# Token rows, their squares and small tables pinned in the instruction order, and transposed operands fetched four k-tiles at a time, in a one-core encoder block

## Chip, core and metric

The kernel runs on one core of one Trainium2 chip. The metric is the device time of one execution in microseconds; three runs give a median. A profiled execution beside them gives the span of the instructions, the busy time of each engine and the trace.

The engines are TensorE (PE; its weight loads are PEld), VectorE (DVE), ScalarE (ACT), GpSimd (POOL) and SyncE (SP). SP and ACT issue the transfers of this kernel; a transfer stands in the instruction stream of the engine that issues it, in that engine's order.

## What is computed

One layer of an encoder block on 256 tokens of width 2048 in float32, cut to what matters:

```python
h = rms_norm(x, g_mix)
proj = h @ w_in                      # q/k/v of mixers A and B, q of mixer C, three gates
oa = dilated windows (3 groups x 2 heads, relative bias), merged by their denominators
ob = grouped-query attention (6 query heads, 2 key/value heads), axial rotary
mkv = rms_norm(mem, g_mem) @ w_mem_kv    # 256 memory tokens -> keys, values of mixer C
oc = cross attention of 4 heads into mkv
merged = sum over branches of sigmoid(gate) * (o_branch @ w_branch)
x = x + merged @ w_o
hf = rms_norm(x, g_ffn) @ w_ffn_in
x = x + (silu(hf[..., :D_FF]) * hf[..., D_FF:]) @ w_ffn_out
```

`rms_norm` divides each token's row by the root of its mean square and multiplies by a gain per channel. The kernel takes these apart. The gain per channel is multiplied into the transposed operand (channels on partitions); the factor per token is applied to the product afterwards. So a product of `mem` can begin before the sums of squares of its rows are known; only what is made from the product needs them.

## The kernel before

**Products.** Every matrix product goes through `product(src, lhs, nk, head, beside)`. It makes 256 tokens x 512 output columns in two PSUM banks (128 tokens each) from `nk` k-tiles of 128 channels. Weights come from memory by SP (`load`, L139 to L148) into one of three buffers `raw` of four k-tiles. `split` (L72) turns a raw float32 tile into two float32r parts: ACT rounds it to `hi`, DVE computes `lo = src - hi`. For weights these are `whi` and `wlo`, four buffers each, two k-tiles per buffer. Each k-tile takes six matmuls, three for each half of the tokens: hi x hi, hi x lo, lo x hi (L172 to L174).

**Transposed operands.** `load_T` (L179) makes the left operand of the products from `memT` or `xT`, which lie transposed in memory. `get(k)` fetches two k-tiles (256 KB) on ACT's queue into `rawT`, which has two buffers, and splits them with the channel gain (L78 on ACT, L79 on DVE). The product asks for them through `lhs(k)`.

**Side work.** Beside the products, generators ("jobs") are advanced by `tick()`, which is called after each k-tile. A job yields the number of k-tiles after which it wants to go on; at most one job advances per tick. The jobs of the opening are:

- `row_sums` (L198): loads the token rows in four tiles `rows` of 128 x 1024 (512 KB each) by SP, squares each on ACT with a sum along the row (L206), and from the sums makes the factor per token (`row_scale`, a chain of small DVE operations). It adds its name to `known`.
- `constants` (L241): three small tables by SP, `gh` (head gains), `rope`, `relb`.
- `fetch` (L249): asks for all of `xT` in steps of two k-tiles, ahead of the first product that reads it.
- `take_slots` (L289): takes a finished product out of PSUM: squares per head (`sq`), then, when the row factors are `known`, the scaled heads `y`, gains, rotary, transposes (`hT`) and splits.
- `biases` and `attend`: tables of relative bias, and the attention of each head.

**Order.** The opening runs two products of `memT` with the two column blocks of `w_mem` (16 k-tiles each), then eight products of `xT` with `w_qkv`. The sums of the mem rows start at k-tile 6 of the first product, those of the x rows at k-tile 0 of the first `w_qkv` product, with pace 3:

```python
first = product(a["w_mem"][0], memT, KT, (1, 1) + (2,) * 7, {6: row_sums(a["mem"], r_m, 3, "mem")})
start(constants())
start(take_slots(first, MEM_SLOTS[:4], r_m, "mem", nc.vector))
start(fetch(xT, 2))
```

The written order is not the order on the chip. The kernel is traced with `schedule_with_timeline_sim=True`: after tracing, a scheduler orders each engine's instructions by a simulated timeline and keeps only the dependences. An instruction that needs nothing but a free buffer, such as a load, can be placed far ahead of where it was written. `tc.keep_in_program_order(ins)` adds one edge: `ins` stays behind the instruction that was traced just before it on the same engine. It adds no wait for that instruction's end, and it does not keep later instructions from passing.

**Buffers.** The pool `mid` has five slots of 4 KB per partition with the common tag `s4`; `rows`, `y`, `sq`, `rot`, `pT`, `row` and later `sg`, `sa` and `junk` share them. The two buffers of `rawT` lie in the pool `wp` and hold 2 KB per partition each.

Of the kernel before, what the change touches and what calls it, by code (L numbers as in the profile page):

```python
# [11 lines left out]
F32 = mybir.dt.float32  # L12
F32R = mybir.dt.float32r
I32 = mybir.dt.int32
AF = mybir.ActivationFunctionType
# [3 lines left out]
P = 128  # L19
S = 256  # L20
T = S // P
D = 2048
KT = D // P
HD = 128
# [12 lines left out]
BUCKETS, MAX_DIST = 32, 1024  # L37
# [13 lines left out]
def encoder_block(ctx: ExitStack, tc: tile.TileContext, a: dict, out: bass.AP):  # L51
    nc = tc.nc
    const = ctx.enter_context(tc.tile_pool(name="const", bufs=1))
    wp = ctx.enter_context(tc.tile_pool(name="wp", bufs=3))
    big = ctx.enter_context(tc.tile_pool(name="big", bufs=11))
    mid = ctx.enter_context(tc.tile_pool(name="mid", bufs=5))
    small = ctx.enter_context(tc.tile_pool(name="small", bufs=4))
    dram = ctx.enter_context(tc.tile_pool(name="dram", bufs=1, space=bass.MemoryType.DRAM))
    pmm = ctx.enter_context(tc.tile_pool(name="pmm", bufs=4, space=bass.MemoryType.PSUM))
# [2 lines left out]
    def s8(shape, name, dt=F32R, pool=None):  # L62
        return (pool or big).tile(shape, dt, name=name, tag="s8")

    def s4(shape, name, dt=F32):
        return mid.tile(shape, dt, name=name, tag="s4")

    def at_bank(name):
        return pat.tile([P, NC], F32, name=name, tag="at")


    def split(hi, lo, src, scale=None):  # L72

        if scale is None:
            nc.scalar.activation(hi, src, AF.Copy)  # L75
            nc.vector.tensor_sub(lo, src, hi.bitcast(F32))  # L76
        else:
            nc.scalar.activation(hi, src, AF.Copy, scale=scale)  # L78
            nc.vector.scalar_tensor_tensor(lo, src, scale, hi.bitcast(F32), op0=ALU.mult, op1=ALU.subtract)  # L79
# [33 lines left out]
    def advance(job):  # L113

        try:
            lag = next(job[1])
            job[0] = now[0] + (lag or 1)
            return lag is not None
        except StopIteration:
            side.remove(job)  # L120
            return True

    def start(steps):

# [14 lines left out]
    def load(src, k0, nk):  # L139

        raw = wp.tile([P, LOAD, NC], F32, name="raw")
        if nk % PK:
            c = k0 % PK * NC
            nc.sync.dma_start(out=raw[:, 0], in_=src[k0 // PK][:, c:c + NC])
        else:
            nc.sync.dma_start(out=raw[:, :nk].rearrange("p (u k) n -> p u (k n)", k=PK),
                              in_=src[k0 // PK:(k0 + nk) // PK].rearrange("u p n -> p u n"))
        return raw  # L148

    def product(src, lhs, nk, head=(), beside={}):  # L150


        ps = [pmm.tile([P, NC], F32, name="mm") for _ in range(T)]
        k0 = 0
        while k0 < nk:
            n = head[0] if head else min(LOAD, nk - k0)
            head = head[1:]
            if k0 in beside:
                start(beside[k0])
            lhs(k0)  # L160
            raw = load(src, k0, n)
            for b in range(0, n, PK):
                m = min(PK, n - b)
                hi = wp.tile([P, PK, NC], F32R, name="whi", bufs=4)
                lo = wp.tile([P, PK, NC], F32R, name="wlo", bufs=4)
                split(hi[:, :m], lo[:, :m], raw[:, b:b + m])
                for i in range(m):
                    k = k0 + b + i
                    xh, xl = lhs(k)
                    for t in range(T):  # L170
                        c = slice(t * P, (t + 1) * P)
                        nc.tensor.matmul(ps[t], lhsT=xh[:, c], rhs=hi[:, i], start=(k == 0), stop=False)  # L172
                        nc.tensor.matmul(ps[t], lhsT=xh[:, c], rhs=lo[:, i], start=False, stop=False)  # L173
                        nc.tensor.matmul(ps[t], lhsT=xl[:, c], rhs=hi[:, i], start=False, stop=(k == nk - 1))  # L174
                    tick()
            k0 += n
        return ps

    def load_T(src, g, tag):  # L179

        tiles = [s8([P, 4, 2, S], tag) for _ in range(KT // 4)]
        have = set()

        def get(k):
            k0 = k // 2 * 2
            tl = tiles[k // 4]
            if k0 not in have:
                have.add(k0)
                raw = wp.tile([P, 2, S], F32, name="rawT", bufs=2)
                nc.scalar.dma_start(out=raw, in_=src[k0 // 2].rearrange("p (k s) -> p k s", s=S))  # L190
                for i in range(k0, k0 + 2):
                    split(tl[:, i % 4, 0], tl[:, i % 4, 1], raw[:, i - k0], g[:, i:i + 1])
            return tl[:, k % 4, 0], tl[:, k % 4, 1]
        return get

# [2 lines left out]
    def row_sums(src, r, pace, name):  # L198

        ss = small.tile([P, T, 2], F32, name="rss", bufs=1)  # L200
        for t in range(T):
            for h in range(2):
                rows = s4([P, D // 2], "rows")
                nc.sync.dma_start(out=rows, in_=src[t * P:(t + 1) * P, h * (D // 2):(h + 1) * (D // 2)])
                yield pace
                nc.scalar.activation(rows, rows, AF.Square, accum_out=ss[:, t, h:h + 1])  # L206
        sr = small.tile([P, T], F32, name="ss", bufs=1)
        nc.vector.tensor_reduce(sr, ss, axis=AX.X, op=ALU.add)
        row_scale(sr, r)
        known.add(name)  # L210

    def transposed(src, dst, g=None):

        for h in range(2):
            tp = at_bank("tp")
            for k in range(2):
                for t in range(T):
                    nc.tensor.transpose(tp[:, k * S + t * P:k * S + (t + 1) * P],  # L218
                                        src[t][:, (2 * h + k) * P:(2 * h + k + 1) * P], ident)
# [17 lines left out]
    gh = const.tile([P, 6, HD], F32, name="gh")  # L237
    rope = const.tile([P, 2, T, HD // 2], F32, name="rope")
    relb = const.tile([P, A_HEADS], F32, name="relb")

    def constants():  # L241
        v = a["g_heads"]
        nc.sync.dma_start(out=gh, in_=bass.AP(tensor=v.tensor, offset=v.offset, ap=[[0, P], [HD, 6], [1, HD]]))
        yield 1
        nc.sync.dma_start(out=rope, in_=a["rope"])
        nc.vector.memset(relb[:64], NEG)
        nc.sync.dma_start(out=relb[:BUCKETS], in_=a["rel_bias"])

    def fetch(get, pace):  # L249
        for k in range(0, KT, 2):  # L250
            get(k)
            yield pace
# [173 lines left out]
    scales = const.tile([P, 3, 2, T], F32, name="scales")  # L426
    r_m, r_x, r_f = (scales[:, i] for i in range(3))
    memT = load_T(a["memT"], gT[:, 1], "memT")
    xT = load_T(a["xT"], gT[:, 0], "xT")
    memT(0)  # L430
    first = product(a["w_mem"][0], memT, KT, (1, 1) + (2,) * 7, {6: row_sums(a["mem"], r_m, 3, "mem")})
    start(constants())
    start(take_slots(first, MEM_SLOTS[:4], r_m, "mem", nc.vector))
    start(fetch(xT, 2))
    start(take_slots(product(a["w_mem"][1], memT, KT, (2,) * 8), MEM_SLOTS[4:], r_m, "mem"))
    oT = [s8([P, 4, 2, S], f"oT{i}") for i in range(3)]
    ol = lambda k: (oT[k // 4][:, k % 4, 0], oT[k // 4][:, k % 4, 1])
    for c in range(8):
        sums = {} if c else {0: row_sums(a["x"], r_x, 3, "x")}
        start(take_slots(product(a["w_qkv"][c], xT, KT, beside=sums), SLOTS[4 * c:4 * c + 4], r_x))  # L440
        if c == 0:
            start(biases())
# [28 lines left out]
    x = [s8([P, D], f"x{t}", F32) for t in range(T)]  # L471
# [20 lines left out]
    for c0, c1 in ((0, 6), (6, KF // 4)):  # L492
        hT = []
        for n in range(c0, c1):
            ap = product(a["w_ffn_a"][n], x1l, KT)
# [7 lines left out]
            tl = s8([P, 2, 4, S], "hT", pool=tail if n % 6 < 4 and n < 6 or n > 8 else None)  # L503
# [91 lines left out]
```

## Time and profile before

| | |
|---|---|
| runs | 1437.47, 1437.15, 1437.45 us; median 1437.45 |
| profiled execution | 1438.22 us, span of its instructions 1436.4 us |
| busy in the span | PE 1416.7, PEld 1170.0, DVE 781.2, ACT 667.2, POOL 78.8 us |
| moved by DMA | 276.98 MB, mean 193 GB/s |
| granted TensorE clock, mean | 0.998 |
| instructions | 16231 |

Times in rows of the profile are microseconds from the start of the span. A timeline row reads: start, duration, engine (an engine with a q, such as SPq, is its sequencer, here issuing a transfer), line, operation, output<-inputs, count; in brackets the idle time of the engine before it and what ended that. A row of a table by stage reads: stretch, length, busy time and number of instructions of PE, PEld, DVE, ACT and POOL, the granted TensorE clock, the mean busy share of the DMA engines, GB/s. A row of waits reads: who waited, for whom, total us, times, longest. A DMA row reads: what, queue, count, KB each, median us from issue to landing. A duration of a matmul is longer than the distance to the next one, since matmuls are pipelined.

### The profile page before, as it was taken

How to read it: one execution, taken by the hardware profiler on the slowest of the kernel's cores; microseconds unless marked ns; L12 is line 12 of the kernel's file. 1: busy time of each engine (PE TensorE's matmuls, PEld its weight loads, DVE VectorE, ACT ScalarE, POOL GpSimd, SP SyncE). 2: the span in 40 equal slices, each digit the busy share in tenths (PEclk: the TensorE clock that was granted, in tenths of full speed). 3: DMA queues.
4: the chain of work that ended last, by engine and by line, in shares of the span. 5: the costliest groups of instructions: out<-in, count | busy, mean ns of one | idle time of the engine just before them, and what ended most of it. 6: DMA issues, size and time to landing. Idle time of an engine off the chain costs nothing.

```text
span 1436.4 us, 16231 instructions
## 1 busy us (share of the span) xinstructions
PE 1416.7 (99%) x6422; PEld 1170.0 (81%) x6422; DVE 781.2 (54%) x912; ACT 667.2 (46%) x860; POOL 78.8 (5%) x146
## 2 busy tenths in 40 slices
PE   6999999999999999999999999999999999999998
PEld 4778788888888888888888888888888888888887
DVE  5677766744555555555644555545444445554543
ACT  6676555644444444444444444444333444444432
POOL 0013642200000000000000000000000000000000
PEclk9999999999999999999999999999999999999999
DMA  8876445465555556555555555565555555556562
GB/s 294 282 248 204 147 153 173 160 222 197 196 192 194 176 189 213 184 187 177 183 197 186 194 177 204 176 205 177 203 179 203 187 194 179 202 177 204 192 218 88
DMA packets 75772, 276.98 MB, mean 193 GB/s; under 512 B 5232, under 2 KB 7792, under 8 KB 75440
## 3 DMA queue, kind: packets, MB, share of 16 engines
q1 hardware_dynamic: 73248, 271.73, 56.0%
q10 hardware_dynamic: 2448, 4.22, 0.8%
q8 instruction: 50, 0.82, 0.2%
q14 instruction: 26, 0.21, 0.0%
HBM read 273.05 MB, written 2.88 MB: 192 GB/s over the span
## 4 chain that ended last, share of the span: by engine, by line
PE 92%; DMA 3%; POOL 2%; ACT 1%; issue 1%; DVE 1%; SPq 0%; ACTq 0%; DVEq 0%; POOLq 0%
PE mm L173 29%; PE mm L172 29%; PE mm L174 29%; PE tp L218 1%; DMA rawT<-in_xT 1%; DMA rows<-in_x 1%; DMA rows<-in_mem 1%; POOL rot L337 1%; POOL rot L340 1%; POOL rtmp L338 1%; ACT whi L75 0%; PE pT L396 0%; ACT rows L206 0%; PE hT L346 0%; POOL y L320 0%
## 5 line engine op out<-in xcount | busy, mean ns | idle before, releaser
L76 DVE TENSOR_TENSOR wlo<-raw,whi 128x1024 fp32r<-128x1024 f32 (+1 forms) x497 | 614.7, 1239 | 584.9 <-ACT whi L75 582.6
L75 ACT ACTIVATE whi<-raw 128x1024 fp32r<-128x1024 f32 (+1 forms) x497 | 525.5, 1061 | 642.6 <-PE mm L174 616.6
L174 PE MATMUL mm<-whi,x1T 128*128 128x512 f32 x704 | 274.8, 390 | 0.0
L172 PE MATMUL mm<-whi,x1T 128*128 128x512 f32 x704 | 274.8, 390 | 0.0
L173 PE MATMUL mm<-wlo,x1T 128*128 128x512 f32 x704 | 274.1, 389 | 0.0
L173 PE MATMUL mm<-wlo,xT 128*128 128x512 f32 x640 | 250.2, 391 | 1.0 <-DVE wlo L76 1.0
L172 PE MATMUL mm<-whi,xT 128*128 128x512 f32 x640 | 250.5, 392 | 0.1
L174 PE MATMUL mm<-whi,xT 128*128 128x512 f32 x640 | 249.5, 391 | 0.0
L173 PEld LDWEIGHTS mm<-wlo,x1T 128*128 128x128 f32 x704 | 132.2, 188 | 27.2
L174 PEld LDWEIGHTS mm<-whi,x1T 128*128 128x128 f32 x704 | 132.2, 188 | 27.1
L172 PEld LDWEIGHTS mm<-whi,x1T 128*128 128x128 f32 x704 | 132.2, 188 | 26.9
L173 PEld LDWEIGHTS mm<-wlo,xT 128*128 128x128 f32 x640 | 120.2, 188 | 26.1 <-DVE wlo L76 1.4
L172 PEld LDWEIGHTS mm<-whi,xT 128*128 128x128 f32 x640 | 120.1, 188 | 25.3 <-issue 0.8
L174 PEld LDWEIGHTS mm<-whi,xT 128*128 128x128 f32 x640 | 120.2, 188 | 24.4
L173 PE MATMUL mm<-wlo,hT 128*128 128x512 f32 x352 | 137.8, 391 | 0.0
L172 PE MATMUL mm<-whi,hT 128*128 128x512 f32 x352 | 137.7, 391 | 0.0
L174 PE MATMUL mm<-whi,hT 128*128 128x512 f32 x352 | 137.0, 389 | 0.0
L172 PEld LDWEIGHTS mm<-whi,hT 128*128 128x128 f32 x352 | 66.1, 188 | 14.4
L174 PEld LDWEIGHTS mm<-whi,hT 128*128 128x128 f32 x352 | 66.1, 188 | 14.3
L173 PEld LDWEIGHTS mm<-wlo,hT 128*128 128x128 f32 x352 | 66.1, 188 | 13.5
L173 PE MATMUL mm<-wlo,mT 128*128 128x512 f32 x128 | 50.8, 397 | 0.0
L172 PE MATMUL mm<-whi,mT 128*128 128x512 f32 x128 | 50.5, 395 | 0.0
(123 smaller groups left out, 997.5 us busy)
## 6 DMA issues: line engine op xcount, KB each, us to landing
raw<-in_w_gate SPq DMA_DIRECT2D x48, 1024.0 KB, 5.0
raw<-in_w_ffn_a SPq DMA_DIRECT2D x44, 1024.0 KB, 5.0
raw<-in_w_ffn_b SPq DMA_DIRECT2D x44, 1024.0 KB, 5.0
raw<-in_w_ffn_out SPq DMA_DIRECT2D x44, 1024.0 KB, 5.0
raw<-in_w_qkv SPq DMA_DIRECT2D x32, 1024.0 KB, 5.1
raw<-in_w_o SPq DMA_DIRECT2D x16, 1024.0 KB, 5.0
raw<-in_w_br SPq DMA_DIRECT2D x8, 1024.0 KB, 4.9
raw<-in_w_mem SPq DMA_DIRECT2D x15, 512.0 KB, 4.9
```

Of the source, the lines that this page charges most:

```text
L75: nc.scalar.activation(hi, src, AF.Copy)
L76: nc.vector.tensor_sub(lo, src, hi.bitcast(F32))
L172: nc.tensor.matmul(ps[t], lhsT=xh[:, c], rhs=hi[:, i], start=(k == 0), stop=False)
L173: nc.tensor.matmul(ps[t], lhsT=xh[:, c], rhs=lo[:, i], start=False, stop=False)
L174: nc.tensor.matmul(ps[t], lhsT=xl[:, c], rhs=hi[:, i], start=False, stop=(k == nk - 1))
L218: nc.tensor.transpose(tp[:, k * S + t * P:k * S + (t + 1) * P], src[t][:, (2 * h + k) * P:(2 * h + k + 1) * P], ident)
L337: nc.gpsimd.tensor_mul(ov[:, :, :, c], xv[:, :, :, c], cs[0])
L338: nc.gpsimd.tensor_mul(tmp[:, :n], xv[:, :, :, 1 - c], cs[1])
L340: op(ov[:, :, :, c], ov[:, :, :, c], tmp[:, :n])
```

## The change

Five things, all in the opening:

1. `ordered` (that is, `tc.keep_in_program_order`) is put around the loads of the token rows, their squares, the three tables and the fetches of the transposed operands.
2. `row_sums` is written so that a row tile's load is issued one step ahead of the square of the tile before it; pace 4 in place of 3. The mem sums start at k-tile 8 in place of 6. `constants` yields 8 k-tiles after its first table in place of 1.
3. `get` fetches a quad of four k-tiles as two transfers of 256 KB into one `s4` slot `rawT`; the splits of each k-tile stay where they were. With `fetch=True` it only fetches.
4. A job `ahead` fetches quads in advance: of `memT` from k-tile 2 with pace 3, of `xT` from the end of the first product with pace 4. `fetch` begins 4 k-tiles later.
5. `mid` has six slots in place of five; the two `rawT` buffers in `wp` go.

```diff
-    mid = ctx.enter_context(tc.tile_pool(name="mid", bufs=5))
+    mid = ctx.enter_context(tc.tile_pool(name="mid", bufs=6))
+    ordered = tc.keep_in_program_order
@@ product
-            if k0 in beside:
-                start(beside[k0])
+            for job in beside.get(k0, ()):
+                start(job)
@@ load_T
-        have = set()
-        def get(k):
-            k0 = k // 2 * 2
-            tl = tiles[k // 4]
+        raws, have = {}, set()
+        def get(k, fetch=False):
+            k0, q = k // 2 * 2, k // 4
+            tl = tiles[q]
+            if q not in raws:
+                raw = raws[q] = s4([P, 4, S], "rawT")
+                for u in range(2):
+                    ordered(nc.scalar.dma_start(out=raw[:, 2 * u:2 * u + 2],
+                                                in_=src[2 * q + u].rearrange("p (k s) -> p k s", s=S)))
+            if fetch:
+                return
             if k0 not in have:
                 have.add(k0)
-                raw = wp.tile([P, 2, S], F32, name="rawT", bufs=2)
-                nc.scalar.dma_start(out=raw, in_=src[k0 // 2].rearrange("p (k s) -> p k s", s=S))
                 for i in range(k0, k0 + 2):
-                    split(tl[:, i % 4, 0], tl[:, i % 4, 1], raw[:, i - k0], g[:, i:i + 1])
+                    split(tl[:, i % 4, 0], tl[:, i % 4, 1], raws[q][:, i % 4], g[:, i:i + 1])
@@ row_sums
-        for t in range(T):
-            for h in range(2):
-                rows = s4([P, D // 2], "rows")
-                nc.sync.dma_start(out=rows, in_=...)
-                yield pace
-                nc.scalar.activation(rows, rows, AF.Square, accum_out=ss[:, t, h:h + 1])
+        parts = [(t, h) for t in range(T) for h in range(2)]
+        rows = []
+        for i in range(len(parts) + 1):
+            if i < len(parts):
+                t, h = parts[i]
+                rows.append(s4([P, D // 2], "rows"))
+                ordered(nc.sync.dma_start(out=rows[i], in_=...))
+            if i:
+                t, h = parts[i - 1]
+                ordered(nc.scalar.activation(rows[i - 1], rows[i - 1], AF.Square, accum_out=ss[:, t, h:h + 1]))
+            yield pace
@@ constants: the three loads in ordered(...); yield 8 for yield 1
@@ fetch
+        yield 4
@@ opening
+    def ahead(get, pace):
+        for k in range(0, KT, 4):
+            get(k, True)
+            yield pace
+
     memT(0)
-    first = product(..., (1, 1) + (2,) * 7, {6: row_sums(a["mem"], r_m, 3, "mem")})
+    first = product(..., (1, 1) + (2,) * 7, {2: [ahead(memT, 3)], 8: [row_sums(a["mem"], r_m, 4, "mem")]})
     start(constants())
     start(take_slots(first, MEM_SLOTS[:4], r_m, "mem", nc.vector))
+    start(ahead(xT, 4))
     start(fetch(xT, 2))
...
-        sums = {} if c else {0: row_sums(a["x"], r_x, 3, "x")}
+        sums = {} if c else {0: [row_sums(a["x"], r_x, 4, "x")]}
```

More of the change, by code (lines that the diff above doesn't have):

```diff
@@ L200, in row_sums @@
         ss = small.tile([P, T, 2], F32, name="rss", bufs=1)
-        for t in range(T):
-            for h in range(2):
-                rows = s4([P, D // 2], "rows")
-                nc.sync.dma_start(out=rows, in_=src[t * P:(t + 1) * P, h * (D // 2):(h + 1) * (D // 2)])
-                yield pace
-                nc.scalar.activation(rows, rows, AF.Square, accum_out=ss[:, t, h:h + 1])
+        parts = [(t, h) for t in range(T) for h in range(2)]
[4 more added lines that the diff above has]
+                rows.append(s4([P, D // 2], "rows"))
+                ordered(nc.sync.dma_start(out=rows[i],
+                                          in_=src[t * P:(t + 1) * P, h * (D // 2):(h + 1) * (D // 2)]))
+            if i:
+                t, h = parts[i - 1]
+                ordered(nc.scalar.activation(rows[i - 1], rows[i - 1], AF.Square, accum_out=ss[:, t, h:h + 1]))
+            yield pace
         sr = small.tile([P, T], F32, name="ss", bufs=1)
@@ L242, in constants @@
         v = a["g_heads"]
-        nc.sync.dma_start(out=gh, in_=bass.AP(tensor=v.tensor, offset=v.offset, ap=[[0, P], [HD, 6], [1, HD]]))
-        yield 1
-        nc.sync.dma_start(out=rope, in_=a["rope"])
+        ordered(nc.sync.dma_start(out=gh, in_=bass.AP(tensor=v.tensor, offset=v.offset, ap=[[0, P], [HD, 6], [1, HD]])))
+        yield 8
+        ordered(nc.sync.dma_start(out=rope, in_=a["rope"]))
         nc.vector.memset(relb[:64], NEG)
-        nc.sync.dma_start(out=relb[:BUCKETS], in_=a["rel_bias"])
+        ordered(nc.sync.dma_start(out=relb[:BUCKETS], in_=a["rel_bias"]))
     def fetch(get, pace):
+        yield 4
         for k in range(0, KT, 2):
@@ L429, in encoder_block @@
     xT = load_T(a["xT"], gT[:, 0], "xT")
+    def ahead(get, pace):
+        for k in range(0, KT, 4):
+            get(k, True)
+            yield pace
     memT(0)
-    first = product(a["w_mem"][0], memT, KT, (1, 1) + (2,) * 7, {6: row_sums(a["mem"], r_m, 3, "mem")})
+    first = product(a["w_mem"][0], memT, KT, (1, 1) + (2,) * 7, {2: [ahead(memT, 3)], 8: [row_sums(a["mem"], r_m, 4, "mem")]})
     start(constants())
     start(take_slots(first, MEM_SLOTS[:4], r_m, "mem", nc.vector))
+    start(ahead(xT, 4))
     start(fetch(xT, 2))
```

## Prediction

> **What bounds the kernel now.** I read the page's busy table and its slices first, then the table by stage for the whole span, then TensorE's own waits, then the timeline of the first 70 us with all engines and queues.
>
> ```profile
> PE 1416.7 (99%) x6422; PEld 1170.0 (81%) x6422; DVE 781.2 (54%) x912; ACT 667.2 (46%) x860; POOL 78.8 (5%) x146
> PE   6999999999999999999999999999999999999998
> ...
> 0.00:62.00 62.00, 49.54 (x194) 38.91 (x195) 37.92 (x82) 38.49 (x68) 0.70 (x6) 0.94 0.85 285
> 62.00:140.00 78.00, 76.88 (x365) 61.61 (x365) 54.17 (x100) 50.58 (x101) 19.09 (x33) 1.00 0.72 234
> 140.00:180.00 40.00, 38.27 (x197) 32.07 (x195) 30.33 (x52) 21.64 (x52) 25.52 (x37) 1.00 0.47 157
> 180.00:400.00 220.00, 220.00 (x1054) 184.34 (x1053) 131.12 (x170) 113.92 (x174) 33.53 (x71) 1.00 0.54 184
> ...
> 1200.00:1400.00 200.00, 200.00 (x895) 165.40 (x894) 98.47 (x88) 83.80 (x85) 0.00 (x0) 1.00 0.58 198
> ```
>
> Columns of the stage rows: stretch, its length, busy PE, weight load, DVE, ACT, POOL with counts, granted clock, DMA share, GB/s. From 180 to 1400 us (first and last of six rows) TensorE has no idle time: nothing that the edit does there can gain, and there is slack on every other engine. The opening is different: 62 us hold 49.54 us of TensorE, at a clock of 0.94. Two stages behind it lack 1.1 and 1.7 us. So the case is decided in the first two products (both w_mem column blocks, 32 k-tiles).
>
> ```profile
> PE mm L172 <- ACT memT L78: 11.9, 2, 6.2
> PE hT L346 <- POOL rot L340: 1.7, 2, 1.4
> PE mm L173 <- DVE wlo L76: 1.0, 1, 1.0
> PE mm L174 <- DVE memT L79: 0.2, 1, 0.2
> ...
> 2.12 3.04 SPq L204 DMA_DIRECT2D rows<-in_mem  x4
> 5.30 1.48 SPq L146 DMA_DIRECT2D raw<-in_w_mem  x2
> 8.51 0.34 ACTq L190 DMA_DIRECT2D rawT<-in_memT  x1
> 9.71 1.04 ACT L206 ACTIVATE rows<-rows 128x1024 f32<-128x1024 f32 x1
> 13.36 0.61 PE L174 MATMUL mm<-whi,memT 128*128 128x512 f32 x2
> 14.17 1.06 ACT L206 ACTIVATE rows<-rows 128x1024 f32<-128x1024 f32 x1 [3.33 <-DMA rows<-in_mem]
> 16.27 1.04 ACT L206 ACTIVATE rows<-rows 128x1024 f32<-128x1024 f32 x1
> 17.30 1.99 ACT L75 ACTIVATE whi<-raw 128x1024 fp32r<-128x1024 f32 x2
> 19.20 0.90 ACT L78 ACTIVATE memT<-rawT,gT 128x256 fp32r<-128x256 f32 x2
> 19.75 0.80 PE L172 MATMUL mm<-whi,memT 128*128 128x512 f32 x1 [5.77 <-ACT memT L78]
> ```
>
> Of the 11.9 us, 6.2 are the start (first operands must land) and 5.77 are one hole. The rows show its making. In the code the row sums start at k-tile 6, but SP issued all four row loads at 2.12 us, ahead of the weights of k-tiles 4 to 7 (5.30). ACT's queue has the squares early as well: it sits 3.33 us for the second row tile, squares until 17.30, splits two weight tiles, and only then splits memT for k-tile 4, which TensorE wanted at 13.97.
>
> The hole has a second price, the clock.
>
> ```profile
> 14.00:19.00 5.00, 0.00 (x0) 0.00 (x0) 1.36 (x8) 4.83 (x8) 0.00 (x0) 0.84 1.01 389
> 20.00:22.00 2.00, 1.82 (x4) 0.93 (x4) 1.97 (x8) 0.09 (x1) 0.00 (x0) 0.50 0.49 113
> 22.00:24.00 2.00, 1.94 (x5) 1.56 (x6) 0.93 (x6) 1.06 (x2) 0.00 (x0) 0.50 0.71 252
> 24.00:26.00 2.00, 2.00 (x10) 1.64 (x9) 1.98 (x4) 1.74 (x3) 0.00 (x0) 0.94 0.71 284
> ```
>
> For some 4.5 us behind the hole the granted clock is 0.50: 4 and 5 matmuls begin in 2 us where 10 do at 0.94. The start has the same half pace, 0.43 us between two starts, though the clock column says 1.00 there; that one stays.
>
> ```profile
> 7.18 0.63 PE L172 MATMUL mm<-whi,memT 128*128 128x512 f32 x1
> ...
> 7.61 0.63 PE L173 MATMUL mm<-wlo,memT 128*128 128x512 f32 x1
> ```
>
> **The change, part by part.** First the ceiling. The steady pace of these products:
>
> ```profile
> 54.78 0.39 PE L172 MATMUL mm<-whi,memT 128*128 128x512 f32 x1
> 61.36 0.39 PE L174 MATMUL mm<-whi,memT 128*128 128x512 f32 x1
> 61.58 0.39 PE L172 MATMUL mm<-whi,xT 128*128 128x512 f32 x1
> ```
>
> Thirty matmuls start between 54.78 and 61.58, 0.2267 us each, so a k-tile of six takes 1.360 us. K-tile 3 ends with the pair that starts at 13.36; the next could start at about 13.81. The 28 remaining mem k-tiles without a hole would bring the first xT matmul to 13.81 + 28 x 1.360 = 51.9 instead of 61.58. **Ceiling: 9.7 us**: 5.8 hole, about 2.1 clock, the rest waits under 1 us that follow it.
>
> *Rows and squares pinned.* No instruction is removed or added. Row tile 0 is now issued behind the weights of k-tiles 6 and 7, its square stands four k-tiles later, and so on; the last mem square moves from 17 us to behind k-tile 24 of 32.
>
> ```profile
> L206 ACT ACTIVATE rows<-rows x8: 1039/1048/1086, 9.7 to 75.5; 128x1024 f32<-128x1024 f32 x8
> L206 ACT ACTIVATION_READ_ACCUMULATOR rows<-rows x8: 185/186/225, 10.7 to 76.4; 128x1 f32 x8
> rows<-in_mem SPq DMA_DIRECT2D x4, 512.0 KB, 8.0
> ```
>
> A square with its read costs about 1.14 us of ACT (next start to start), once in four k-tiles of 5.44 us. What hides it: per two k-tiles (2.72 us) ACT has one weight split (1.06) and one memT pair (0.90), so 3.9 us in four k-tiles, and 5.1 with the square. That is 94% of ACT while memT is being split; afterwards it is easy. If the cover goes, a square costs TensorE at most its 1.14 us, four of them 4.6. A row load takes 8.0 us to land and has four k-tiles plus the queue's lead of three weight buffers; SP does not wait on it, only ACT at the square.
>
> *Small tables pinned.* gh, rope and relb (0.5 MB in all, 384 + 128 + 0.8 KB) leave the 7.7 to 11 us stretch and are issued between the products. Before, they lay among full-rate transfers; at the 389 GB/s of the row from 14 us they free 1.3 us of transfer there. I count that inside the ceiling. Nobody needs gh before the first y has been scaled:
>
> ```profile
> 60.13 0.86 ACT L313 ACTIVATE y<-mm,hf 128x128 f32<-128x128 f32 x3
> ```
>
> *Transposed operands by fours.* Still eight transfers of 256 KB per operand, now two per quad, both on ACT's queue. Bytes and issues do not change. What changes is where a fetch stands: quads 1, 2 and 3 of memT go behind the weight splits of k-tiles 3, 7 and 11, and the splits that need them follow almost directly. This is the price I cannot read off, so I bound it by landings:
>
> ```profile
> rawT<-in_memT ACTq DMA_DIRECT2D x1, 256.0 KB, 6.1
> rawT<-in_memT ACTq DMA_DIRECT2D x8, 256.0 KB, 4.3
> rawT<-in_xT ACTq DMA_DIRECT2D x1, 256.0 KB, 2.6
> ```
>
> (slowest of the stretch of interest, median of eight, fastest.) With 4.3: quad 1 issued at 8.5 (as the fetch in the rows above) lands 12.8, split 0.5 later, needed 13.81: 0.3 allowed for the vector half. ACT then has two memT pairs and a weight split (2.8 us, its last part overlapped by the issue), so quad 2 leaves at 15.0, lands 19.3, usable 19.8; needed at 19.25 (+0.3): 0.3 to 0.5. Quad 3 leaves at 22.5 if ACT splits in written order, lands 26.8, usable 27.3, needed at 25.5: 1.8; if ACT does the weight splits while it waits for quad 2, as it did at 17.30, nothing. I take 1.0. Sum 1.8. With 2.6 the sum is about 0. With 6.1 in written order it grows from quad to quad: 1.3, then 2.85, then 3.9, in all 8.0. I take the median: it comes from fetches among weight loads alone, as these will be, while 6.1 had row tiles and tables in flight with it.
>
> xT's quads start 16 k-tiles ahead of use, paced by four; no cost. They share the six slots with rows, y, sq; counting lifetimes in written order I get at most six live at once, so I count no slot wait (the rival below does). The sixth slot later costs and gains nothing: TensorE is full there. POOL's queue gets nothing and loses nothing.
>
> *Transfers as a second ceiling.* By the first xT matmul must have landed: memT 2.1, w_mem 8.4, mem rows 2.1, xT 2.1, tables 0.5, first w_qkv load 1.05 MB: 16.3 MB. The opening row moved 285 GB/s at a share of 0.85, so 335 at 1.0: 48.6 us, plus 2.5 until the first bytes, 51.1. That is under 51.9, with hardly a microsecond to spare; I put 0.4 us of weight waits on it.
>
> Sum: 9.7 - 1.8 - 0.4 = **7.5 us**. The later waits (1.1 us around 65 us, 1.7 around 150) I leave as they are: the first came from a burst of row loads that is now spread, the second from POOL's rotation, which moves along. The profiled execution took 1438.22 us around a span of 1436.4; it becomes 1430.7 around 1428.9. It lies 0.77 above the median of 1437.45, so the median becomes 1430.0.
>
> **The rivals.**
> *A: fetches wait in full (6.1 us, written order).* For: the fetch at 8.51 took 6.1, and row tiles 0 and 1 still travel next to quads 2 and 3. Against: the four row loads that filled the engines then are gone. Gain 9.7 - 8.0 = 1.7, so 1435.8. Its last hole, 3.9 us, lies between the 0.99 us idle at 65 us that cost no clock and the 5.77 that did; if it does, 2.1 more: 1437.9, no change.
>
> ```profile
> 65.91 0.50 PE L173 MATMUL mm<-wlo,xT 128*128 128x512 f32 x1 [0.99 <-DVE wlo L76]
> ```
>
> The Trainium skill ("TensorE: Matmul & The Clock Gate", Part 1) has the clock halve after an idle window of about 3.4 us. By it a hole of 2.85 would be spared and one of 3.9 could be hit; no row here lies between 0.99 and 5.77.
>
> *B: fetches land fast (2.6).* For: the row tiles and tables no longer stand in front. Stalls near 0, and the 65 us wait goes as well: 9.7 + 1.0 less 0.4 of weights, 10.3, so 1427.2. Against: the DMA share is still 1.01 between 14 and 19 us in the row above. The Trainium skill ("DMA: Bandwidth & Descriptors", Queues, rings and completion order) says that each DMA engine takes turns between queues packet by packet, so a fetch on ACT's queue would not stand behind SP's backlog but have half the rate: 0.26 MB at 0.2 MB per us is 1.3 us above the bare latency, an estimate that leads to B. The trace speaks against: 6.1 us at 8.51.
>
> *C: a slot wait blocks a queue (slower).* Fetches used to have two slots of their own; now an xT fetch on ACT's queue can wait for a slot held by y, freed only by the head transposes. Everything on ACT stands behind it. ACT leads TensorE by at most four weight tiles, so three more when it stops: 3 x 2.72 = 8.2 us of cover. It costs more than it gains by 0.2% when the wait exceeds 8.2 + 7.5 + 2.9 = 18.6 us; a wait from k-tile 20 to 37 (23 us) would give 1437.45 - 7.5 + 15 = 1445. For: y is held across the w_mem[1] product. Against: six slots suffice by my count.
>
> *D: it doesn't do what it says.* A pin keeps an instruction behind its predecessor, but others can still pass it; if the order of ACT's splits ends up as poor as before, the hole stays, with transfers merely shifted: 1437, within 0.2%. Against: a square can't pass its predecessor, and it was squares that made the hole.
>
> **How the numbers follow.** 0.2% is 2.9 us, about what a measurement tells from no change; the bounds are 1434.6 and 1440.3. Forecast (1428.5 to 1432.5) 0.52; B (below 1428.5) 0.18; A 0.18, of which 0.10 with only some of its waits ends under 1434.6 and 0.08 above; D 0.05; C 0.07. Faster: 0.52 + 0.18 + 0.10 = 0.80; same: 0.08 + 0.05 = 0.13; slower 0.07. The range goes from B's 1427.2 to A's 1435.8, leaving about 0.07 below and 0.13 above.
>
> **What would show it.** Right: row loads at or after 6.8 us on SP's queue; no square on ACT before about 14 us; the 5.77 us hole gone and one stretch of half pace only, the first, as now (0.43 us between starts); the first xT matmul at 54 (51.9 + 2.2); small holes, if any, at k-tiles 8 and 12, charged to memT, with rawT transfers behind them. Wrong: holes above 2 us charged to memT (A), no half clock and xT at 52 (B), an xT fetch or row load whose issue stands for many microseconds with ACT or SP idle behind it (C), squares still ahead of k-tile 8's splits (D).

## The result, and the profile after

The changed kernel takes 1445.03 us (median of 1444.14 to 1447.34) against 1437.46 before: ratio 1.0053, 95% interval 1.0035 to 1.0070. It is 7.6 us slower, where 7.5 us faster was forecast. The profiled execution took 1444.70 us around a span of 1442.9, 6.5 more than before.

The table by stage first (columns as before):

```profile
0.00:62.00 62.00, 48.94 (x192) 38.76 (x192) 38.35 (x80) 40.30 (x67) 0.70 (x6) 0.97 0.87 294
62.00:140.00 78.00, 72.93 (x322) 57.87 (x322) 45.59 (x84) 42.67 (x87) 23.25 (x38) 0.96 0.70 227
140.00:180.00 40.00, 38.25 (x209) 31.64 (x208) 33.20 (x62) 25.84 (x58) 19.41 (x32) 1.00 0.41 134
180.00:400.00 220.00, 220.00 (x1056) 184.31 (x1057) 132.12 (x176) 115.16 (x179) 32.87 (x71) 1.00 0.52 182
```

From 180 us on TensorE is as full as before. The first 62 us hold about as little TensorE work as before, and the stage from 62 to 140 now lacks 5.1 us where it lacked 1.1. TensorE's waits, and the two holes in its timeline:

```profile
PE mm L174 <- ACT memT L80: 10.1, 2, 6.4
PE mm L174 <- DVE V L81: 7.9, 1, 7.9
PE hT L361 <- POOL rot L355: 1.4, 2, 0.9
```

```profile
29.39 0.79 PE L174 MATMUL mm<-whi,memT 128*128 128x512 f32 x1 [3.61 <-ACT memT L80]
67.00 0.76 PE L174 MATMUL mm<-whi,xT 128*128 128x512 f32 x1 [7.90 <-DVE V L81]
```

The old hole of 5.77 us at 14 us is gone. There is one of 3.61 at k-tile 12, and one of 7.90 in front of the first `w_qkv` product. The second does not wait for an operand: `V L81` reads the product `w_mem[1]` out of PSUM. A product needs two of four PSUM banks; the two `w_mem` products held all four. TensorE goes on 0.14 us after a pair of these reads ends; seven of the eight reads by VectorE are done then, which by the program's order empties one of that product's two banks, and the last comes later:

```profile
66.06 0.80 DVE L81 SCALAR_TENSOR_TENSOR V<-mm,scales,V 128x128 fp32r<-128x128 f32 x2
68.83 0.35 DVE L81 SCALAR_TENSOR_TENSOR V<-mm,scales,V 128x128 fp32r<-128x128 f32 x1 [1.98 <-ACT V L80]
```

Behind the hole the clock is halved:

```profile
59.00:67.00 8.00, 0.10 (x1) 0.03 (x1) 7.62 (x22) 5.43 (x13) 0.00 (x0) 0.78 1.00 311
67.00:69.00 2.00, 2.00 (x5) 1.61 (x6) 0.17 (x1) 1.80 (x7) 0.38 (x1) 0.50 1.01 412
69.00:71.00 2.00, 2.00 (x8) 1.58 (x7) 0.18 (x1) 0.00 (x0) 2.00 (x1) 0.68 0.94 336
```

Eight matmuls take the 3.43 us from 67.00 to 70.43 in place of 1.81: 1.6 us more. Why the banks were held is read from SP's, ACT's and VectorE's timelines, here in order of time:

```profile
11.10 0.42 SPq L215 DMA_DIRECT2D rows<-in_mem  x1
19.49 0.90 SPq L215 DMA_DIRECT2D rows<-in_mem  x2
20.54 0.33 SPq L257 DMA_DIRECT2D gh<-in_g_heads  x1
34.28 0.42 SPq L215 DMA_DIRECT2D rows<-in_mem  x1
...
43.76 1.05 ACT L219 ACTIVATE rows<-rows 128x1024 f32<-128x1024 f32 x1
45.03 0.15 DVE L222 TENSOR_REDUCE ss<-rss 128x2 f32<-128x4 f32 x1
55.95 0.16 DVE L109 COPY scales<-rs_y 128x2 f32<-128x2 f32 x1
57.99 0.16 DVE L322 TENSOR_TENSOR hss<-hss,scales 128x8 f32<-128x8 f32 x1
65.98 0.16 DVE L324 TENSOR_TENSOR hf<-rs_y,scales 128x8 f32<-128x8 f32 x1
66.37 2.17 ACT L328 ACTIVATE y<-mm,hf 128x128 f32<-128x128 f32 x8
```

And four of these points in the kernel before, where the fourth row tile was issued by 5.2 us:

```profile
16.27 1.04 ACT L206 ACTIVATE rows<-rows 128x1024 f32<-128x1024 f32 x1
22.77 0.17 DVE L107 COPY scales<-rs_y 128x2 f32<-128x2 f32 x1
48.63 0.16 DVE L307 TENSOR_TENSOR hss<-hss,scales 128x8 f32<-128x8 f32 x1
57.45 0.17 DVE L309 TENSOR_TENSOR hf<-rs_y,scales 128x8 f32<-128x8 f32 x1
```

The last mem square moved from 16.3 to 43.8 us. The factor per token (`scales`) came at 56.0 in place of 22.8, the factor per head (`hf`) at 66.0 in place of 57.5. The chain for the head factor begins with the row `hss`, the first reader of the row factor. Without the head factor `y`, which empties the first product, cannot run. `V`, which empties the second, needs only the row factor; that was there at 56.0, but the second product itself ended at 59.1, and then its reads were drawn out among weight splits until 66.9. So TensorE, done with the second product at 59.1, found no free bank. Each of the two chains is about a dozen VectorE operations of 0.16 us, but they take 11 and 8 us; VectorE's timeline has weight and xT splits between them.

In sum: the first xT matmul 5.4 us later (67.00 against 61.58), 1.6 us of half clock behind it, less the old 0.99 us wait at 65 us: 6.0 of the 6.5 us.

### The profile page after: what moved, and what is told of

Read it like the earlier page. It is cut to its first block, busy times and chain, and to the rows that moved or that the text cites. A ratio compares the mean times of both kernels' runs of the same rounds, so it can differ in the third digit from the quotient of the medians.

```text
span 1442.9 us, 16232 instructions
## 1 busy us (share of the span) xinstructions
PE 1418.7 (98%) x6422; PEld 1171.2 (81%) x6422; DVE 780.7 (54%) x912; ACT 668.9 (46%) x860; POOL 76.2 (5%) x146
## 4 chain that ended last, share of the span: by engine, by line
PE 90%; DMA 4%; DVE 3%; POOL 1%; ACT 1%; issue 1%; SPq 0%; ACTq 0%; DVEq 0%; POOLq 0%
PE mm L175 29%; PE mm L174 29%; PE mm L176 29%; DMA raw<-in_w_mem 2%; DVE wlo L78 1%; PE tp L232 1%; DMA rawT<-in_memT 1%; ACT whi L77 0%; DMA rawT<-in_xT 0%; ACT y L328 0%; PE pT L411 0%; DVE pr L401 0%; DMA relb<-in_rel_bias 0%; DMA flat<-row 0%; PE hT L361 0%
```

## The experiments

**Theory 1:** the mem factors come too late, and the banks stay held. **Theory 2:** pinned row loads hold up the weights on SP's queue. **Theory 3:** the fetches by fours and the shared slots cost the time. The first four kernels part them.

*mem_factor_given* takes the need for the factor away:

```diff
+    dummy = const.tile([P, 2, T], F32, name="dummy")
+    nc.vector.memset(r_m, 1.0)
+    known.add("mem")
...
-    8: [row_sums(a["mem"], r_m, 4, "mem")]
+    8: [row_sums(a["mem"], dummy, 4, "sums")]
```

> The changed kernel, but the row factor of the mem tokens is set to one at the start and nothing waits for the sums of the mem rows; their loads, squares and chain stay and write a table that nobody reads (left out: the true factor). Theory 1 (the mem factor comes late, so neither pair of product banks is free when the first w_qkv product is due): the 7.9 us hole in front of it and the 1.6 us at half clock behind it go, about 1435.5 us; the 3.6 us hole inside the first product stays. Theory 2 (pinned row loads hold up the weight loads on SP's queue): nothing changes there, 1443 or more. Theory 3 (fetches by fours and shared slots): the same, 1443 or more.

Measured: 1435.01 us, ratio 0.9974 (0.9964 to 0.9984). There is no hole in front of the first xT matmul at 58.2 us; a 4.19 us hole inside the first product is left (10.0 less the 5.8 of the start, in the row below). The head factor in VectorE's timeline, and TensorE's waits:

```profile
51.57 0.17 DVE L324 TENSOR_TENSOR hf<-rs_y,scales 128x8 f32<-128x8 f32 x1
```

```profile
PE mm L174 <- ACT memT L80: 10.0, 2, 5.8
PE hT L361 <- POOL rot L355: 3.2, 2, 1.7
```

Ten microseconds (1445.0 against 1435.0) hang on the mem factor alone; the row loads stood where they stood. Theory 1 holds for the large hole, and theories 2 and 3 do not explain it.

*sums_from_6_pace_3*:

```diff
-    8: [row_sums(a["mem"], r_m, 4, "mem")]
+    6: [row_sums(a["mem"], r_m, 3, "mem")]
```

> The changed kernel with the mem sums started at k-tile 6 with pace 3, as before, in place of 8 and 4; all pins and the fetches by fours stay. Written order has the factor known after k-tile 18 in place of 28. Theory 1: ten k-tiles or 13.6 us earlier is more than the 7.9 us that were short, so the large hole goes: 1434 to 1437 us. Theory 2: the row loads stand earlier among the weights, 1445 to 1448. Theory 3: no change, 1445.

Measured: 1435.51 us, ratio 0.9987 (0.9973 to 1.0000). (The written place is k-tile 21, not 18: the new `row_sums` yields once more before the factor.) Its profiled execution took 1443.6 us, 8 above the median, so its trace is not set beside the others here. Start and pace alone are worth 9.5 us, which is the size of the large hole with its half clock (7.9 + 1.6).

The change in two halves, *rows_part_alone* (pins, new `row_sums`, tables; operands still by twos) and *quads_alone* (the new `load_T`, `ahead`, six slots; old `row_sums` and `constants`). Each takes the lines of the change that it names:

```diff
 rows_part_alone, against the kernel before
+ ordered(...) on row loads, squares, tables; square one step behind the load; constants: yield 8
-    {6: row_sums(a["mem"], r_m, 3, "mem")}
+    {8: [row_sums(a["mem"], r_m, 4, "mem")]}
 quads_alone, against the kernel before
-    mid bufs=5, rawT: 2 x [P, 2, S] in wp
+    mid bufs=6, rawT: [P, 4, S] in s4, ordered fetches, ahead(memT, 3), ahead(xT, 4), fetch: yield 4
```

> The kernel before with only the part on rows and tables (pins on row loads, squares and tables, loads one step ahead, start 8, pace 4); operands fetched by twos into two slots of their own, five shared slots. Theory 1: the loss is all here, with the hole in front of the first w_qkv product: 1442 to 1447 us. Theory 2: likewise 1442 to 1447, but with the holes inside the two w_mem products, charged to weights. Theory 3: no loss, 1430 to 1437.

> The kernel before with only the fetches by fours (four-k-tile slots among six shared ones, pinned fetches, fetches ahead); rows, squares and tables as before, without pins. Theories 1 and 2: no loss, 1435 to 1439 us, with the old 5.8 us hole that early squares make. Theory 3: the loss is here, 1442 to 1447.

Measured: rows part alone 1449.88 us, ratio 1.0084 (1.0069 to 1.0099); fours alone **1431.76 us, ratio 0.9952 (0.9937 to 0.9967)**. The first is worse than the whole change, the second is better than both kernels by 6 us or more. TensorE's holes behind the start, rows part first, then fours alone:

```profile
18.75 0.50 PE L174 MATMUL mm<-whi,memT 128*128 128x512 f32 x1 [1.96 <-ACT memT L80]
28.17 0.50 PE L174 MATMUL mm<-whi,memT 128*128 128x512 f32 x1 [1.75 <-ACT memT L80]
68.48 0.77 PE L174 MATMUL mm<-whi,xT 128*128 128x512 f32 x1 [9.56 <-DVE V L81]
```

```profile
14.96 0.50 PE L174 MATMUL mm<-whi,memT 128*128 128x512 f32 x1 [0.36 <-ACT memT L80]
26.68 0.50 PE L174 MATMUL mm<-whi,memT 128*128 128x512 f32 x1 [0.54 <-ACT memT L80]
54.02 0.62 PE L174 MATMUL mm<-whi,xT 128*128 128x512 f32 x2
```

With fours alone xT starts at 54.0 us, unheld (the profiled execution was the fastest of four, 1429.0 us), and the old hole is gone without a pin on any row or square. SP's order shows how: the row tiles no longer jump ahead.

```profile
8.12 0.33 SPq L212 DMA_DIRECT2D rows<-in_mem  x1
10.47 0.33 SPq L148 DMA_DIRECT2D raw<-in_w_mem  x1
10.85 0.42 SPq L212 DMA_DIRECT2D rows<-in_mem  x1
13.53 6.18 SPq L148 DMA_DIRECT2D raw<-in_w_mem  x3
19.77 0.92 SPq L212 DMA_DIRECT2D rows<-in_mem  x2
```

**What makes the lateness?** Candidates: the chains in VectorE's queue (1a), the row tiles (1b), the pins. *chain_on_gpsimd* (`row_scale` and the head chain of the first product on GpSimd) and *rows_not_pinned* (no `ordered` on row loads and squares):

```diff
 chain_on_gpsimd
-        row_scale(sr, r)
+        row_scale(sr, r, nc.gpsimd if name == "mem" else nc.vector)
-    start(take_slots(first, MEM_SLOTS[:4], r_m, "mem", nc.vector))
+    start(take_slots(first, MEM_SLOTS[:4], r_m, "mem"))
 rows_not_pinned
-                ordered(nc.sync.dma_start(out=rows[i], ...))
+                nc.sync.dma_start(out=rows[i], ...)
-                ordered(nc.scalar.activation(rows[i - 1], ...))
+                nc.scalar.activation(rows[i - 1], ...)
```

> The changed kernel with the two small chains that follow the mem sums (row factor, then head factor; some 12 operations of 0.16 us each) on GpSimd in place of VectorE; loads, squares and their places stay. In the changed kernel the last mem square ends at 44.9 us, the row factor is there at 56.0 and the head factor at 66.0, though the operations are 2 us each in sum; between them VectorE does weight and xT splits that wait for transfers. Theory 1a (the chain is drawn out in VectorE's queue): row factor by 50, head factor by 55, the 7.9 us hole and its 1.6 us of half clock gone, 1434 to 1437 us. Theory 1b (the row tiles themselves come too late): at least half of the hole stays, 1440 to 1445.

> The changed kernel without the pins on row loads and squares; start 8, pace 4 and all else stay. If the pins make the lateness: rows come early again, the large hole goes, 1431 to 1437 us. If the later start, the slower pace and the six shared slots make it: the row loads stand where they did, 1442 to 1447.

Measured: 1444.79 us, ratio 1.0050 (1.0035 to 1.0065), and 1445.34, ratio 1.0057 (1.0042 to 1.0072). Neither helps. On GpSimd the head factor comes at 62.5 us in place of 66.0, but single operations on tiny tiles take up to 2.35 us there:

```profile
49.39 2.35 POOL L100 TENSOR_TENSOR rs_y<-rs_y,rs_t 128x2 f32<-128x2 f32 x1
62.46 0.20 POOL L324 TENSOR_TENSOR hf<-rs_y,scales 128x8 f32<-128x8 f32 x1
65.87 0.80 PE L174 MATMUL mm<-whi,xT 128*128 128x512 f32 x1 [4.50 <-ACT whi L77]
```

So this run does not part 1a from 1b: the chains were hardly faster there (row factor at 54.0 in place of 56.0). Without the row pins SP's row loads stand in the same order among the weights (11.6, 17.5 and 31.9 us), and the hole is 9.49. Beside the fetches by fours the row pins change the time by nothing that can be told.

*tables_not_pinned* (`constants` as before):

```diff
-        ordered(nc.sync.dma_start(out=gh, ...))
-        yield 8
+        nc.sync.dma_start(out=gh, ...)
+        yield 1
```

> The changed kernel with the three tables as before (no pins, step 1). In the changed kernel gh leaves at 20.5 us, 0.1 us before memT's last quad at 20.65, which lands 8 us later and makes the 3.6 us hole with 1.5 us or more of half clock behind it; with fetches by fours alone, gh left at 2.1 us and the hole was 0.5. Theory on gh: hole below 1.5 us, first w_qkv product due 3 to 5 us earlier; but the row factor then still comes late and may eat it: 1440 to 1445 us. Rival (the two row tiles at 19.5 us delay the quad): hole of 3 to 4 us stays.

Measured: 1442.15 us, ratio 1.0028 (1.0018 to 1.0038): 2.9 us better. The hole at k-tile 12 is 2.96, not below 1.5. So gh at 20.5 us makes at most a small part of it; the rival (row tiles beside the quad) is not shown either, because with fours alone the same two tiles left at 19.8 us and the hole was 0.54.

*quads_without_pins* (fours alone, no `ordered` on the fetches):

```diff
-                    ordered(nc.scalar.dma_start(out=raw[:, 2 * u:2 * u + 2], ...))
+                    nc.scalar.dma_start(out=raw[:, 2 * u:2 * u + 2], ...)
```

> The kernel before with the fetches by fours, but without the pins on them. That version with pins ran in 1431.8 us. If the larger fetch and the shared slots are what took the old 5.8 us hole away: 1430 to 1434 us. If it was the pins on the fetches: the hole is back, 1435 to 1439.

Measured: 1432.98 us, ratio 0.9969 (0.9955 to 0.9983). The pins on the fetches are not what gained.

**Is the written place the whole loss?** *early_sums_free_tables* is the changed kernel with sums at 6, pace 3, and free tables; *row_pins_at_old_place* the kernel before with pins, tables and new `row_sums`, at 6 and 3; *late_sums_no_pins* the kernel before with the new `row_sums` at 8 and 4 and no pin.

```diff
 early_sums_free_tables, against the changed kernel
-    8: [row_sums(a["mem"], r_m, 4, "mem")]
+    6: [row_sums(a["mem"], r_m, 3, "mem")]
+ constants as before
 row_pins_at_old_place, against rows_part_alone
-    8: [row_sums(a["mem"], r_m, 4, "mem")]
+    6: [row_sums(a["mem"], r_m, 3, "mem")]
 late_sums_no_pins, against rows_part_alone
- ordered(...) on row loads, squares and tables; constants: yield 8
+ constants as before
```

> The changed kernel with the mem sums at k-tile 6, pace 3, and the tables as before; pins on rows and squares, loads one step ahead and fetches by fours stay. If the later written place of the mem sums and of the tables is the whole loss: as fast as fetches by fours alone (1431.8), so 1430 to 1434 us, and the row pins are worth nothing either way. If the row pins cost something by themselves: 1436 or more.

> The kernel before with pins on row loads, squares and tables and the loads one step ahead, but mem sums at k-tile 6 with pace 3; operands by twos. If lateness of the written place makes the loss and the pins only hold things there: the old 5.8 us hole goes (no square ahead of its place) and no large hole comes in front of the first w_qkv product, 1431 to 1437 us. If the pins cost by themselves: 1442 or more.

> The kernel before with the row sums of the change (k-tile 8, pace 4, loads one step ahead) without any pin; tables as before, operands by twos. In the order that results, SP issues three mem row tiles at once at the start and the fourth only behind ten more weight loads, in the second product. If the last row tile decides: the row factor comes as late as in the changed kernel or later, with a hole of 6 us or more in front of the first w_qkv product, 1442 to 1450 us, plus part of the old hole. If the pins make the loss: about 1437.

Measured: 1438.47 us, ratio 1.0002 (0.9993 to 1.0011); 1441.93, ratio 1.0023 (1.0011 to 1.0035); 1453.70, ratio 1.0110 (1.0089 to 1.0131). The third is as theory 1 has it: SP takes three row tiles at 2.1 us and the fourth at 41.8, the head factor comes at 68.1, and TensorE stands 11.32 us. The first came out in the range given for a cost of the pins, the second in neither range. Their xT starts in good time (57.5 and 60.7 us), but two waits come later in all three, here of the first:

```profile
134.41 0.69 PE L361 MATMUL hT<-ident,rot 128*128 128x128 f32 x2 [2.56 <-POOL rot L355]
169.35 0.50 PE L174 MATMUL mm<-whi,xT 128*128 128x512 f32 x1 [2.92 <-DVE V L81]
```

That left open whether pins or the rewritten sums cost the 6.7 us over fours alone. Three kernels on top of fours alone decide it: *fours_sums_late* (only 8 and 4), *fours_row_pins* (only pins on row loads and squares), *fours_ahead_no_pins* (the first kernel above without those pins).

```diff
 fours_sums_late
-    6: [row_sums(a["mem"], r_m, 3, "mem")]
+    8: [row_sums(a["mem"], r_m, 4, "mem")]
 fours_row_pins
-    nc.sync.dma_start(out=rows, ...)
+    ordered(nc.sync.dma_start(out=rows, ...))
-    nc.scalar.activation(rows, rows, AF.Square, ...)
+    ordered(nc.scalar.activation(rows, rows, AF.Square, ...))
```

> Fetches by fours alone (1431.8 us) with one number pair changed: mem sums at k-tile 8 with pace 4 in place of 6 and 3; no pins on rows, squares or tables, old row_sums. The fourth mem row tile is then issued four weight loads later. If the later place makes the late factor: head factor after 57 us in place of 49.0, the first w_qkv product held behind it, 1437 to 1445 us. If the pins make it: 1430 to 1434.

> Fetches by fours alone (1431.8 us) with pins on the row loads and squares added and nothing else: start 6, pace 3, loads not one step ahead, tables free. SP's order of the mem rows is the same as without. If the pins cost by themselves: 1436 to 1440 us. If they are inert here: 1430 to 1434.

> The kernel of 1438.5 us (changed kernel, sums at k-tile 6, pace 3, tables free) without the pins on rows and squares; loads one step ahead, the extra pace before the factor and x pace 4 stay. If its 6.7 us over fetches by fours alone come from the row pins: 1430 to 1434 us. If they come from the rewritten row sums (factor one pace later, x pace 4): 1436 to 1440.

Measured: 1438.06 us, ratio 0.9997 (0.9987 to 1.0006); 1431.41, ratio 0.9949 (0.9934 to 0.9964); 1439.45, ratio 0.9996 (0.9986 to 1.0007). One pair of numbers costs 6.3 us, the pins nothing, and the rewritten sums with pace 4 for x cost 7.7 us without any pin on the rows, so the reading of the first kernel as a cost of the pins was wrong. Which of the rewriting's parts costs (load one step ahead, factor one pace later, x at pace 4) was not parted. In *fours_sums_late* the head factor came at 60.3 us (fours alone: 49.0):

```profile
33.83 0.42 SPq L212 DMA_DIRECT2D rows<-in_mem  x1
60.27 0.15 DVE L318 TENSOR_TENSOR hf<-rs_y,scales 128x8 f32<-128x8 f32 x1
61.84 0.80 PE L174 MATMUL mm<-whi,xT 128*128 128x512 f32 x1 [3.67 <-ACT y L322]
```

Not all of its 6.3 us is the factor: the hole at k-tile 12 is 2.89 us there (0.54 in fours alone), with half clock behind it (0.50 from 30 to 32 us).

Last, *fours_and_tables_later*, fours alone with the tables pinned from k-tile 4 of the second product on:

```diff
-    start(constants())
-    product(a["w_mem"][1], memT, KT, (2,) * 8)
+    product(a["w_mem"][1], memT, KT, (2,) * 8, {4: [constants()]})
+ ordered(...) on the three tables; yield 2
```

> Fetches by fours alone (1431.8 us) with the three tables moved out of the first product: pinned behind k-tile 4 of the second one. Their 0.5 MB are 1.3 us of transfer in a stretch where the DMA share is about 1. If the small holes left in the first product (0.4 and 0.5 us) come from transfers: 1430 to 1431.5; if the gain is eaten by the tables standing among xT fetches: 1432 to 1434.

Measured: 1431.92 us, ratio 0.9951 (0.9938 to 0.9963): no gain on fours alone. Its hole at k-tile 12 is larger, 2.70 us.

Nine of the kernels side by side. The columns are the issue of the fourth mem row tile, the head factor of the first product, the start of the first xT matmul and the hole in front of it, from the profiled execution, and the median time. The kernel before was run again beside each group and had medians from 1437.5 to 1438.7, so a microsecond between two rows says nothing:

| kernel | row tile 4 | head factor | first xT | hole | us |
|---|---|---|---|---|---|
| fours, row pins | 20.1 | 51.6 | 55.5 | 0.45 | 1431.4 |
| fours alone | 20.3 | 49.0 | 54.0 | none | 1431.8 |
| mem factor given | 34.4 | 51.6 | 58.2 | none | 1435.0 |
| before | 4.5 | 57.5 | 61.6 | none | 1437.5 |
| fours, sums late | 33.8 | 60.3 | 61.8 | 3.7 | 1438.1 |
| tables not pinned | 33.0 | 62.4 | 63.4 | 6.1 | 1442.2 |
| change | 34.3 | 66.0 | 67.0 | 7.9 | 1445.0 |
| rows part alone | 41.2 | 67.9 | 68.5 | 9.6 | 1449.9 |
| late sums, no pins | 41.8 | 68.1 | 70.1 | 11.3 | 1453.7 |

Wherever the head factor comes after 60 us, TensorE stands, and in the rows of this table xT then starts 0.6 to 2 us behind the factor (3.4 us in chain_on_gpsimd, where a weight split came between).

## Why the prediction was wrong

**The step that failed** is "Rows and squares pinned". It moved the last mem square from 17 us to k-tile 24 and priced that only by ACT's time ("a square costs TensorE at most its 1.14 us"). It did not ask who waits for the sum. Behind it stand two chains on VectorE, then `y` and `V`, then the four PSUM banks. In the kernel before, the row factor (22.8 us) had 25.8 us of slack to its first reader (48.6), and the change moved it by 33.2. Behind that reader there was no slack at all: `y` came out at 60.1 to 62.3 us, just as TensorE finished the second product at 61.6 (the row at 60.13, quoted for gh, said so), while the plan was to bring TensorE there 7 us earlier. It was the later written place (k-tile 8, pace 4), and not the pins, that made the sums too late: without the pins the last square stands at 41.0 us and the time is the same (rows_not_pinned). Measured price: 9.5 us (sums_from_6_pace_3) to 10.0 (mem_factor_given).

Of the 15 us between the forecast (1430.0) and the time, the wait for the banks and the half clock behind it make about 9.6. Most of the rest was lost earlier: without the banks the first xT matmul could have started at 59.0 us, where 54.1 was forecast. That is the third quad, below.

**The gain was there**, but was put down to the wrong part. The old opening held 9.7 us more than the ceiling by the working; fours alone reached xT at 54.0 us where the prediction had 54.1 (51.9 + 2.2), in an execution 2.7 us faster than its median. That the two agree is in part luck: another kernel got there, with holes of other sizes. The prediction gave that gain to the pins and a cost of 1.8 us to the fours. The fours take the hole away without the pins, and beside them the row pins are worth nothing (1431.4 with, 1431.8 without; 1445.3 without, 1445.0 with). With operands by twos the pins do break the old hole up, into 1.40 and 2.60 us (row_pins_at_old_place), but the time does not fall: 1441.9. Why the scheduler stops placing the row tiles far ahead with fours was not isolated; that quads and rows now share six slots, so that no four are free at the start, is an argument only.

**The price of the fetches** was taken as 0.3, 0.3 to 0.5 and 1.0 us for quads 1, 2 and 3. Measured in the change: none, none and 3.6 us, with 1.7 more of half clock behind it. The two transfers of the third quad landed in 8.9 us (median), beyond the slow end of 6.1 that was taken:

```profile
rawT<-in_memT ACTq DMA_DIRECT2D x2, 256.0 KB, 8.9
gh<-in_g_heads SPq DMA_DIRECT2D x1, 384.0 KB, 8.7
```

The hole at k-tile 12 was 0.5 to 4.2 us over the kernels with fours (two had 2.1 and 2.6 us near 16.5 us instead). No single edit accounts for it: free tables took 0.65 us off it in the change, while on fours alone it is 2.70 with the tables moved later and 0.54 without. Its cause stays open. By the estimate under rival B, the turn-taking between queues that the Trainium skill states ("DMA: Bandwidth & Descriptors", Queues, rings and completion order) would have let this quad land early; its transfers took as long as `gh`, issued on the other queue 0.1 us before them.

**Small tables** were counted as a gain inside the ceiling; free tables were 2.9 us faster in the change, 3.0 slower with early sums, and later ones made no difference with fours alone.

**The rivals.** C had the sign and, by accident, the time (1445). Its mechanism, a queue standing at a slot, does not show: ACT's longest idle time in the changed opening is 3.28 us, and that is for a transfer of xT. A's waits on quads came true for one quad, with the half clock it named (0.58 and 0.57 from 29 to 33 us). D is half true: the pins did little, but the rest of the change did much. The case that happened, late factors holding all product banks, was not among the rivals.

**The fast side.** Without the late sums the change is at 1435.5 us; what differs over the remaining 3.7 us to fours alone is the pinned tables, the rewritten `row_sums` and x sums at pace 4. They do not add up term by term: the kernel with early sums and free tables was 3.0 slower than the one with early sums alone, with the two late waits shown above, 5.5 us in all, where fours alone has 1.8 there. So the edits reorder the attention stage as well; why is not settled.

## What to carry to other kernels

Before work off the critical path is moved later, follow its result to the last reader, and to the buffer that this reader frees: here a 1 us square decided when PSUM banks came free 23 us later. A chain of tiny operations can cost far more than its durations, if other work stands between them in the queue. When a change has several parts, price and run each alone: here one part gained 6 us and another lost 12, and the sum hid both.

## What the runs showed of the hardware

TensorE's clock fell to half after shorter holes than the prediction reckoned with. One of 2.96 us (tables_not_pinned) was enough; the table by stage, with the clock before the DMA share:

```profile
24.00:28.00 4.00, 1.26 (x6) 0.72 (x4) 2.36 (x2) 2.65 (x5) 0.00 (x0) 1.00 0.97 344
28.00:30.00 2.00, 1.78 (x4) 1.50 (x5) 0.90 (x3) 1.12 (x4) 0.00 (x0) 0.56 0.98 372
30.00:32.00 2.00, 2.00 (x7) 1.55 (x6) 1.54 (x3) 2.00 (x3) 0.00 (x0) 0.58 0.30 115
```

So was one of 1.96 us in rows_part_alone (0.50 in the stage 2 us after it), and in fours_ahead_no_pins one of 1.48 with 0.53 more an instant later. But length alone does not decide. Of two holes of 1.90 us the one in sums_from_6_pace_3 halved the clock and the one in row_pins_at_old_place did not; one of 1.75 did not. In early_sums_free_tables the hole of 2.56 us at 134 us halved the clock and the longer one of 2.92 us at 169 us did not:

```profile
134.00:136.00 2.00, 1.59 (x5) 1.40 (x6) 0.00 (x0) 0.00 (x0) 1.84 (x3) 0.50 0.69 283
170.00:172.00 2.00, 2.00 (x11) 1.61 (x10) 1.85 (x3) 1.09 (x3) 1.92 (x3) 1.00 0.00 0
```

The Trainium skill ("TensorE: Matmul & The Clock Gate", Part 1) gives an idle window of about 3.4 us; the measurement decides, and here single holes of 1.9 to 2.9 us sometimes halved the clock and sometimes did not. What decides is not shown. Where it halved, the loss was about as large as behind a long hole: behind the 2.96 us eight matmuls took 3.52 us (28.22 to 31.74) in place of 1.81, 1.7 us more. The prediction reckoned a clock loss for a hole of 3.9 us only, and so priced shorter ones too low.
